# A hybrid decoder layer on one core: work of GpSimd in the fronts and the last stage put on VectorE and ScalarE, the S5 columns reordered by the gelu, and the merge's gate loads put ahead or on GpSimd's queue

## The chip, the core and the metric

The kernel runs on one core of a Trainium2 chip. A core has TensorE (PE, with its weight loads PEld), VectorE (DVE), ScalarE (ACT), GpSimd (POOL) and SyncE (SP), which issues most transfers. Each engine runs its instructions in the order in which they stand in its program. The metric is the device time in microseconds of one execution.

## What is computed

One layer of a decoder trunk on x of 1024 positions by 1024 channels, float32. Two token-mixing branches, a gated merge, and a gated MLP with a short convolution:

```python
h = rms_norm(x, norm_mix_pre)
proj = h @ w_in
p_rwkv, u_s5, gates = split(proj)          # gates = sigmoid(. + b_gate)
o_rwkv = rwkv7_branch(p_rwkv, ...) @ w_branch_rwkv
o_s5 = s5_branch(u_s5, ...) @ w_branch_s5  # ends: y = gelu(y); y * sigmoid(y @ w_glu + b_glu)
mixed = (g_rwkv * o_rwkv + g_s5 * o_s5) @ w_out
x = x + rms_norm(mixed, norm_mix_post)
f = conv_ffn(rms_norm(x, norm_ffn_pre), w_up, conv_w, conv_b, w_down)
x = x + rms_norm(f, norm_ffn_post)
```

The RWKV-7 branch is a recurrence over positions per head, with decay, key k, value v, receptance r and two vectors made from the normalised key; the S5 branch is a diagonal complex scan. A sigmoid is written as a tanh throughout, so a gate is (t + 1) times the product, with a factor of a half folded elsewhere.

## The kernel before

**Tiling.** Channels stand on the 128 partitions, positions in the columns. The sequence is worked in two halves of 512 positions, th = 0 and th = 1. Every large product is made of three float32r matmuls (`mm3_steps`, L172 to L174): the high part of the data by the high part of the weights, low by high, and high by low. The splits are made by a cast on ACT (L226, L156) and a difference on VectorE (L227, L157).

**Order.** TensorE's order is made by hand: a planner (`drive`) puts generators beside each other, and a `yield` in one of them names a modelled duration (the constants T_...), after which its next TensorE step may come. What is not a chain's own step is "fill": wide matmuls of the projections, gates and up-products that are put between. The order of the other engines and queues is made by the framework from priorities, as the data allow.

**The stages, in the time of the profiled run.** The input projection runs first; the RWKV fronts and chains and the S5 scans run beside it and beside the merge: the first half's fronts from about 262 to 322 us, the second half's from 478 to 560, the first half's merge from about 575, and the second half's from about 736 to 830. Up-products and convolution follow to about 1190, the down-product after that, and the outputs at the end.

**A front** (`rwkv_front`, L642 to L735) prepares one group of two units, of 128 channels each, for the chain; a half has two groups, so there are four group fronts in all. Per unit it loads k, tz and ta, then makes four 128x512 arrays: `bk0`, `bk1` (L670, L671, L690, L692, L701, L704) and `ar0`, `ar1` (L691, L702). It takes the key's norm by a small matmul (L677) that ends in `sv` (L682, L683), is spread by ACT (L688) and transposed by TensorE into `kb` (L698). L684 is a running sum over 64 columns, L686 and L687 are its Exps. Then the mask products: four matmul blocks per group (two units, two halves q, L716), each into a pair of PSUM buffers `cz`. There are two such pairs, so a block's matmuls wait until the block two before it has been emptied by VectorE's masked evictions into `gr` (L719, two per block). After the last one the products go out to memory through GpSimd's queue (L728) and come back for an inversion (L773 to L796), and a bonus product is made (L723, L734).

**The chain's end** transposes the result (L916), and ACT scales it into `ld` (L920); it is combined with the gate `TG` and stored as `YR` (L926).

**S5's end** (`s5_y`, `s5_split`, `glu_tile`). YU is loaded with its columns in the order j, n (8 by 64). ACT takes the gelu in place (L1092). The order n, j is needed, so the split's cast (L1097) and difference (L1098) and the product behind the GLU (L1108) work through a strided view.

**The merge.** `gate` (L1111 to L1118) loads the weights `w_br` and the gate `GT` (L1115), makes the product (PSUM `gm` or `mm`), and VectorE multiplies (L1118). `merge` does it for th = 0; `merge_s5` and `merge_rk` for th = 1, where `merge_rk` first loads the chain's `YR` (L1211). These loads are issued on SP's queue, among the loads of weights (L155) and of x (L1230).

**The last stage.** The outputs of th = 0 are made while the down-product's last part runs: ACT scales into a stage buffer (L1604), GpSimd multiplies by the norm (L1605) and adds the residual (L1606). Those of th = 1 come at the end, on VectorE (L1602, and L1606 for five of eight) and GpSimd (L1606 for three).

Of the kernel before, what the change touches and what calls it, by code (L numbers as in the profile page):

```python
# [66 lines left out]
class Kern:  # L67
# [574 lines left out]
    def rwkv_front(self, d, g, th, pt, start):  # L642
# [25 lines left out]
        for e in L:  # L668
            p = e["p"]
            G.tensor_scalar(e["bk1"], c64(e["ta"]), self.ka_h[:, p:p + 1], self.ka_1[:, p:p + 1], ALU.mult, ALU.add)  # L670
            G.tensor_tensor(e["bk1"], e["bk1"], c64(e["k"]), ALU.mult)  # L671
            A.activation(e["kk"], e["k"], AF.Square, scale=self.vec("k_k", p))
# [6 lines left out]
        for u, e in enumerate(L):  # L679
            p, tz = e["p"], e["tz"]  # L680
# [3 lines left out]
            V.tensor_tensor_scan(tz, self.cst("smask"), tz, 0.0, ALU.mult, ALU.add)  # L684
# [3 lines left out]
            A.copy(c64(e["yb"]), y.unsqueeze(2).to_broadcast([128, 8, 64]))  # L688
# [4 lines left out]
            e["r"] = ld(self.RKV[p])  # L693
# [5 lines left out]
        for e in L:  # L699
            r, tz = e["r"], e["tz"]  # L700
            V.scalar_tensor_tensor(e["bk0"], e["bk0"], -0.5, c64(e["kb"]), ALU.mult, ALU.mult)  # L701
            G.tensor_tensor(e["ar1"], c64(r), e["pe"][:, :, 1:65], ALU.mult)  # L702
            G.tensor_tensor(c64(r), c64(r), e["bk1"], ALU.mult)
            G.tensor_tensor(e["bk1"], e["bk1"], c64(tz), ALU.mult)  # L704
# [188 lines left out]
    def rwkv_out(self, ds, th, latency):  # L893
# [18 lines left out]
        for g, d in enumerate(ds):  # L912
# [14 lines left out]
            yield 1.0, 2.5  # L927
# [57 lines left out]
    def shifted_into(self, xs, mt):  # L985
# [3 lines left out]
        def use(th, ps):  # L989
            y = self.shifted(ps, mt, th)  # L990
            if mt == 12:
                nc.scalar.activation(y[0:64], y[0:64], AF.Tanh)
            else:
                nc.scalar.activation(y, y, AF.Tanh, scale=0.5)
                nc.gpsimd.tensor_scalar(y, y, 1.0, 0.5, ALU.add, ALU.mult)
# [4 lines left out]
    def lowrank(self, xs, js):  # L1000

        nc = self.nc
        for j, hb, dst in js:
            w = self.load_w(self.a["w_lr"][j])
            for th in range(2):
                for p in range(4):
# [7 lines left out]
                    if dst is self.TZ:  # L1014
                        nc.gpsimd.tensor_scalar(t, t, 1.0, 1.0, ALU.add, ALU.mult)
# [73 lines left out]
    def s5_y(self, t, b, th):  # L1089

        self.nc.sync.dma_start(t, self.YU[b].rearrange("j c g n -> (c g) j n")[:, :, th * 64:th * 64 + 64])
        self.nc.scalar.activation(t, t, AF.Gelu_apprx_tanh)  # L1092
        return t.rearrange("p j n -> p n j")

    def s5_split(self, hi, lo, y):
        r = [x.rearrange("p (n j) -> p n j", j=8) for x in (hi, lo)]
        self.nc.scalar.copy(r[0], y)  # L1097
        self.nc.vector.tensor_tensor(r[1], y, r[0].bitcast(F32), ALU.subtract)  # L1098

    def glu_tile(self, m, xs, t, y, to):  # L1100
# [5 lines left out]
        t3 = t.rearrange("p (n j) -> p n j", j=8)  # L1106
        nc.scalar.activation(t, ps, AF.Tanh, bias=self.hb["b_glu"][:, m:m + 1], scale=0.5)
        nc.vector.scalar_tensor_tensor(t3, t3, 1.0, y(), ALU.add, ALU.mult)  # L1108
        self.split_half(*to, t)

    def gate(self, j, m, th, br, t, out):  # L1111
# [3 lines left out]
        nc.sync.dma_start(t, self.GT[8 * j + m][:, th * 512:th * 512 + 512])  # L1115
# [15 lines left out]
    def merge(self, mg):  # L1131
# [11 lines left out]
        def inputs():  # L1143
# [808 lines left out]
```

## Time and profile before

| what | us |
|---|---|
| median of 3 runs | 1551.08 |
| lowest and highest of them | 1547.18, 1552.98 |
| the profiled execution, whole | 1552.89 |
| its span in the trace | 1551.1 |
| TensorE busy in it | 1460.4 |
| VectorE busy | 1081.2 |
| ScalarE busy | 687.0 |
| GpSimd busy | 161.1 |

All times of single instructions are from this one profiled execution. A row of a timeline has the start, the duration, the engine, the line, the operation, the tiles it writes and reads, its shape, how many alike are drawn together, and in brackets how long the engine stood idle before it and on what. A row of waits has the total, how often, and the longest. The matmuls of TensorE overlap, so the duration of one (0.39 us for 128x512) is longer than the distance from one start to the next.

### The profile page before, as it was taken

To read this page: it belongs to the slowest core of one execution; us is meant where nothing else is said; L and a number is where in the kernel's file an instruction comes from. 1 tells how busy PE (TensorE), PEld (TensorE's weight loads), DVE (VectorE), ACT (ScalarE), POOL (GpSimd) and SP (SyncE) were. 2 spreads that over 40 slices of the span, in tenths; PEclk is the share of its full clock that TensorE was granted. 3 is DMA by queue.
4 is the path that set the end of the run, shared out by engine and by line. 5 is a ranking of instruction groups with operands and counts; after the bars stand their busy time and mean duration, and the time that the engine had idled before them with its cause. 6 is when DMAs were issued, how large, how long until landed. Compare 5 with 4: busy or idle time off the path is not lost.

```text
span 1551.1 us, 24273 instructions
## 1 busy us (share of the span) xinstructions
PE 1460.4 (94%) x9332; PEld 1194.8 (77%) x9332; DVE 1081.2 (70%) x1733; ACT 687.0 (44%) x1069; POOL 161.1 (10%) x180
## 2 busy tenths in 40 slices
PE   5999899999999798999898999999999999999995
PEld 4787788778878586777776888788888887888774
DVE  6898784745326549447786689777777777697765
ACT  5354442433323444436444446444444444444361
POOL 2120100620103410100000000000000000000006
PEclk9999999999999899899998999999999999999997
DMA  6163342633513464523874444222222226944712
GB/s 208 41 203 118 93 127 100 196 115 113 153 44 107 153 190 143 144 69 94 255 245 161 153 144 137 103 82 82 82 84 88 87 82 203 334 149 134 241 59 108
DMA packets 131107, 210.45 MB, mean 136 GB/s; under 512 B 37696, under 2 KB 43840, under 8 KB 130992
## 3 DMA queue, kind: packets, MB, share of 16 engines
q1 hardware_dynamic: 124208, 188.32, 38.3%
q0 software_dynamic: 5632, 18.49, 3.7%
q10 hardware_dynamic: 1152, 2.10, 0.4%
q8 instruction: 73, 1.20, 0.3%
q14 instruction: 42, 0.34, 0.1%
HBM read 153.28 MB, written 53.48 MB: 133 GB/s over the span
## 4 chain that ended last, share of the span: by engine, by line
PE 69%; DVE 12%; DMA 8%; issue 5%; ACT 4%; POOL 1%; SPq 0%; DVEq 0%; ACTq 0%; POOLq 0%
PE gm L172 8%; PE gm L173 8%; PE gm L174 7%; PE rp L1382 4%; PE rp L1383 4%; PE rp L1384 4%; DMA st<-in_w_down_dram 2%; PE mm L1383 2%; PE mm L1382 2%; PE mm L1384 2%; PE ch L172 2%; PE ch L173 2%; PE ch L174 2%; PE d L1557 2%; PE d L1556 2%
## 5 line engine op out<-in xcount | busy, mean ns | idle before, releaser
L172 PE MATMUL gm<-hh,wh 128*128 128x512 f32 x688 | 284.7, 414 | 14.2 <-DVE hl L1118 8.8
L173 PE MATMUL gm<-hl,wh 128*128 128x512 f32 x688 | 273.4, 397 | 0.2 <-DVE hl L227 0.2
L174 PE MATMUL gm<-hh,wl 128*128 128x512 f32 x656 | 260.0, 396 | 0.0
L157 DVE TENSOR_TENSOR wl<-wf,wh 128x512 fp32r<-128x512 f32 x175 | 123.1, 705 | 116.1 <-ACT wh L156 108.1
L156 ACT CAST wh<-wf 128x512 fp32r<-128x512 f32 x179 | 110.5, 619 | 209.6 <-PE gm L173 129.4
L172 PEld LDWEIGHTS gm<-hh,wh 128*128 128x128 f32 x688 | 132.2, 192 | 49.0 <-DVE hl L1118 10.9
L173 PEld LDWEIGHTS gm<-hl,wh 128*128 128x128 f32 x688 | 132.3, 192 | 26.3 <-issue 1.0
L174 PEld LDWEIGHTS gm<-hh,wl 128*128 128x128 f32 x656 | 125.6, 191 | 27.5
L1557 PE MATMUL d<-xl,wh 128*128 128x512 f32 x308 | 120.2, 390 | 3.5 <-DVE xl L227 3.5
L1556 PE MATMUL d<-xh,wh 128*128 128x512 f32 x308 | 120.1, 390 | 2.1 <-ACT xh L226 2.1
L1558 PE MATMUL d<-xh,wl 128*128 128x512 f32 x308 | 119.9, 389 | 0.0
L1382 PE MATMUL rp<-t,h 128*128 128x512 f32 x216 | 84.4, 391 | 1.4 <-ACT p L1396 1.4
L1384 PE MATMUL rp<-t,l 128*128 128x512 f32 x216 | 84.2, 390 | 0.5 <-DVE l L227 0.5
L1383 PE MATMUL rp<-t,h 128*128 128x512 f32 x216 | 84.1, 389 | 0.0
L1557 PEld LDWEIGHTS d<-xl,wh 128*128 128x128 f32 x308 | 57.8, 188 | 16.5 <-DVE xl L227 4.8
L1556 PEld LDWEIGHTS d<-xh,wh 128*128 128x128 f32 x308 | 57.8, 188 | 14.5 <-ACT xh L226 2.5
L1558 PEld LDWEIGHTS d<-xh,wl 128*128 128x128 f32 x308 | 57.8, 188 | 12.0
L226 ACT CAST h<-r 128x1024 fp32r<-128x1024 f32 x34 | 35.8, 1054 | 61.1 <-PE rp L1383 32.5
L227 DVE TENSOR_TENSOR l<-r,h 128x1024 fp32r<-128x1024 f32 x34 | 41.6, 1224 | 29.2 <-ACT h L226 27.7
L1403 DVE SCALAR_TENSOR_TENSOR y<-zv,vecs,y 128x1023 f32<-128x1023 f32 (+1 forms) x36 | 46.1, 1280 | 8.5 <-ACT y L1401 8.5
L1382 PEld LDWEIGHTS rp<-t,h 128*128 128x128 f32 x216 | 40.5, 188 | 10.8 <-ACT p L1396 2.2
L1384 PEld LDWEIGHTS rp<-t,l 128*128 128x128 f32 x216 | 40.6, 188 | 9.4 <-DVE l L227 1.0
(458 smaller groups left out, 3269.8 us busy)
## 6 DMA issues: line engine op xcount, KB each, us to landing
r<-in_w_up_dram SPq DMA_DIRECT2D x36, 512.0 KB, 3.6
wf<-in_w_in_dram SPq DMA_DIRECT2D x68, 256.0 KB, 3.0
st<-in_w_down_dram SPq DMA_DIRECT2D x55, 256.0 KB, 4.3
st<-ACT SPq DMA_DIRECT2D x44, 256.0 KB, 4.4
wf<-in_w_up_dram SPq DMA_DIRECT2D x36, 256.0 KB, 2.7
ACT<-y POOLq DMA_DIRECT2D x18, 512.0 KB, 2.9
GT<-ev SPq DMA_DIRECT2D x32, 256.0 KB, 2.4
wf<-in_w_br_dram SPq DMA_DIRECT2D x32, 256.0 KB, 3.4
```

What stands on the lines that cost most here:

```text
L156: nc.scalar.copy(h[:, :n], f[:, :n])
L157: nc.vector.tensor_tensor(l[:, :n], f[:, :n], h[:, :n].bitcast(F32), ALU.subtract)
L172: mm(ps, a, xh[k], start=k == 0, stop=False)
L173: mm(ps, a, xl[k], start=False, stop=False)
L174: mm(ps, b, xh[k], start=False, stop=k == n - 1)
L1382: mm(ps, wh[:, c], xh, start=first and k == 0, stop=False, skip_group_check=True)
L1383: mm(ps, wh[:, c], xl, start=False, stop=False, skip_group_check=True)
L1384: mm(ps, wl[:, c], xh, start=False, stop=k == 3, skip_group_check=True)
L1403: V.scalar_tensor_tensor(y[:, lag:], z[:, 0:1024 - lag], self.vec(nme, i), y[:, lag:], ALU.mult, ALU.add)
L1556: mm(ps, wh[:, c], xh[:, x], start=start, stop=False, skip_group_check=True)
L1557: mm(ps, wh[:, c], xl[:, x], start=False, stop=False, skip_group_check=True)
L1558: mm(ps, wl[:, c], xh[:, x], start=False, stop=stop, skip_group_check=True)
```

## The change

Six edits, of one kind or another:

1. In `rwkv_front` the GpSimd operations go: L670 becomes an Identity with scale and bias on ACT, L671 and L702 to L704 go to VectorE. The running sum is moved ahead, the load of r one step ahead, and the spread of the norm (`yb`) ahead of the two Exps. T_BK, the modelled time between the transposes of the norm and the mask products, falls from 7 to 5 us.
2. In the input projection the GpSimd operations L995 and L1015 go to VectorE and ACT.
3. The gelu writes its result in the reordered columns into a buffer of its own; the splits and the product behind the GLU are contiguous. In the first half's merge the four S5 inputs are made in two steps of two.
4. The loads of the gates get a high priority, and for the second half's RWKV gates they are issued on GpSimd's queue, and so are the loads of `YR`.
5. In the last stage the outputs are made in place. Those of th = 0 are made on VectorE alone, six tiles while the last part's evictions start and two after it.
6. The chain's end at th = 1 yields 6.0 in place of 2.5 us of modelled time.

```diff
         for e in L:
-            p = e["p"]
-            G.tensor_scalar(e["bk1"], c64(e["ta"]), self.ka_h[:, p:p + 1], self.ka_1[:, p:p + 1], ALU.mult, ALU.add)
-            G.tensor_tensor(e["bk1"], e["bk1"], c64(e["k"]), ALU.mult)
-            A.activation(e["kk"], e["k"], AF.Square, scale=self.vec("k_k", p))
+            A.activation(e["kk"], e["k"], AF.Square, scale=self.vec("k_k", e["p"]))
+            e["r"] = ld(self.RKV[e["p"]])
+        for e in L:
+            p, tz = e["p"], e["tz"]
+            V.tensor_tensor_scan(tz, self.cst("smask"), tz, 0.0, ALU.mult, ALU.add)
+            A.activation(e["bk1"], c64(e["ta"]), AF.Identity, bias=self.ka_1[:, p:p + 1], scale=self.ka_h[:, p:p + 1])
+            V.tensor_tensor(e["bk1"], e["bk1"], c64(e["k"]), ALU.mult)
         yield 0, T_SQ
...
             V.scalar_tensor_tensor(e["bk0"], e["bk0"], -0.5, c64(e["kb"]), ALU.mult, ALU.mult)
-            G.tensor_tensor(e["ar1"], c64(r), e["pe"][:, :, 1:65], ALU.mult)
-            G.tensor_tensor(c64(r), c64(r), e["bk1"], ALU.mult)
-            G.tensor_tensor(e["bk1"], e["bk1"], c64(tz), ALU.mult)
+            V.tensor_tensor(e["ar1"], c64(r), e["pe"][:, :, 1:65], ALU.mult)
+            V.tensor_tensor(c64(r), c64(r), e["bk1"], ALU.mult)
+            V.tensor_tensor(e["bk1"], e["bk1"], c64(tz), ALU.mult)
...
-            yield 1.0, 2.5
+            yield 1.0, 6.0 if th else 2.5
...
-                nc.gpsimd.tensor_scalar(y, y, 1.0, 0.5, ALU.add, ALU.mult)
+                nc.vector.tensor_scalar(y, y, 1.0, 0.5, ALU.add, ALU.mult)
...
-                        nc.gpsimd.tensor_scalar(t, t, 1.0, 1.0, ALU.add, ALU.mult)
+                        nc.scalar.activation(t, t, AF.Identity, bias=self.ones1, scale=1.0)
...
-        self.nc.scalar.activation(t, t, AF.Gelu_apprx_tanh)
-        return t.rearrange("p j n -> p n j")
+        self.nc.scalar.activation(y.rearrange("p (n j) -> p j n", j=8), t, AF.Gelu_apprx_tanh)
+        return y
...
-        nc.sync.dma_start(t, self.GT[8 * j + m][:, th * 512:th * 512 + 512])
+        with self.tc.high_priority(HPW):
+            (nc.gpsimd if th and not j else nc.sync).dma_start(t, self.GT[8 * j + m][:, th * 512:th * 512 + 512])
...
-            if i == 0:
-                inputs()
+            if i < 2:
+                inputs((2 * i, 2 * i + 1))
...
-            nc.sync.dma_start(y, self.YR[k][:, 512:1024])
+            nc.gpsimd.dma_start(y, self.YR[k][:, 512:1024])
...
-        def outputs(th, src, bc, xs):
-            G = nc.gpsimd
+        def outputs(th, src, bc, xs, part=range(NK)):
             for n, m in enumerate(OUTORD[th]):
-                y = stage(0)[:, 0:512]
-                if th:
-                    V.scalar_tensor_tensor(y, src[m], self.vec("g_ffn_post", m), bc, ALU.mult, ALU.mult)
-                else:
-                    A.activation(y, src[m], AF.Identity, scale=self.vec("g_ffn_post", m))
-                    G.tensor_tensor(y, y, bc, ALU.mult)
-                (V if th and n not in (0, 2, 4) else G).tensor_tensor(y, y, xs[m], ALU.add)
+                if n not in part:
+                    continue
+                y = src[m]
+                V.scalar_tensor_tensor(y, y, self.vec("g_ffn_post", m), bc, ALU.mult, ALU.mult)
+                (nc.gpsimd if th and n in (0, 2, 4) else V).tensor_tensor(y, y, xs[m], ALU.add)
                 nc.sync.dma_start(self.out[m * 128:m * 128 + 128, th * 512:th * 512 + 512], y)
...
-T_KN, T_BK, T_GR, T_NF, T_MT, T_INV, T_LV, T_CH = 7.0, 7.0, 4.0, 5.0, 8.0, 43.0, 1.0, 0.8
+T_KN, T_BK, T_GR, T_NF, T_MT, T_INV, T_LV, T_CH = 7.0, 5.0, 4.0, 5.0, 8.0, 43.0, 1.0, 0.8
```

In the rows of the new order the line numbers are those of the changed file: a front's lines and those of the chain's end stand 2 or 3 higher (L719 is L721, L690 is L693, L682 is L684), the products L671 and L702 to L704 are L675 and L704 to L706, L1115 is L1113 and L1211 is L1213. The order on an engine is set by the planner and the framework, so the diff alone doesn't tell what moves. First, VectorE in the first half's first group, at its mask evictions (before L719, now L721; each pair of `cz` is one block, `ld_`, `bk_591` and `ar_28` belong to the second group's front). Before:

```order
L719 TENSOR_TENSOR gr_2593<-cz_2836,csts 128x4x128
L719 TENSOR_TENSOR gr_2593<-cz_2837,csts 128x4x128
L719 TENSOR_TENSOR gr_2593<-cz_2856,csts 128x4x128
L719 TENSOR_TENSOR gr_2593<-cz_2857,csts 128x4x128
L157 TENSOR_TENSOR wl_3157<-wf_3158,wh_3156 128x512
L978 SCALAR_TENSOR_TENSOR ev_2905<-gm_2823,vecs,ev_2905 128x511
L982 SCALAR_TENSOR_TENSOR ev_2905<-last,vecs,ev_2905 128x1
L719 TENSOR_TENSOR gr_2593<-cz_2929,csts 128x4x128
L719 TENSOR_TENSOR gr_2593<-cz_2930,csts 128x4x128
L719 TENSOR_TENSOR gr_2593<-cz_2949,csts 128x4x128
L719 TENSOR_TENSOR gr_2593<-cz_2950,csts 128x4x128
```

Now, with the first block's pair (cz_2827 and cz_2828) some rows above:

```order
L704 TENSOR_TENSOR ar_2867<-ld_2957,gr_2869 128x8x64
L693 SCALAR_TENSOR_TENSOR bk_591_2868<-ld_2882,ld_2874 128x8x64
L705 TENSOR_TENSOR ld_2957<-ld_2957,bk_591_2868 128x512
L695 SCALAR_TENSOR_TENSOR bk_591_2868<-bk_591_2868,vecs,ld_2878 128x8x64
L706 TENSOR_TENSOR bk_591_2868<-bk_591_2868,ld_2878 128x8x64
L721 TENSOR_TENSOR gr_2593<-cz_2902,csts 128x4x128
L721 TENSOR_TENSOR gr_2593<-cz_2903,csts 128x4x128
L721 TENSOR_TENSOR gr_2593<-cz_2847,csts 128x4x128
L721 TENSOR_TENSOR gr_2593<-cz_2848,csts 128x4x128
L721 TENSOR_TENSOR gr_2593<-cz_2922,csts 128x4x128
L721 TENSOR_TENSOR gr_2593<-cz_2923,csts 128x4x128
```

Before, the four blocks (unit 0's two, unit 1's two) are emptied in their order. Now the second block (cz_2847, cz_2848) is emptied behind the third (cz_2902, cz_2903) and behind products of the second group's front.

Second, VectorE in the second half's first group, at the last of its four evictions and what stands before it now:

```order
L157 TENSOR_TENSOR wl_5532<-wf_5533,wh_5531 128x512
L684 TENSOR_SCALAR sv_5209<-rp_5199 128x8
L706 TENSOR_TENSOR bk_876_5083<-bk_876_5083,ld_5091 128x8x64
L685 RECIPROCAL sv_5209<-sv_5209 128x8
L684 TENSOR_SCALAR sv_5213<-rp_5204 128x8
L705 TENSOR_TENSOR ld_5172<-ld_5172,bk_876_5083 128x512
L685 RECIPROCAL sv_5213<-sv_5213 128x8
L706 TENSOR_TENSOR bk_876_5083<-bk_876_5083,ld_5093 128x8x64
L694 SCALAR_TENSOR_TENSOR ar_5082<-ld_5089,vecs,gr_5084 128x8x64
L695 SCALAR_TENSOR_TENSOR bk_876_5083<-bk_876_5083,vecs,ld_5093 128x8x64
L721 TENSOR_TENSOR gr_4729<-cz_5137,csts 128x4x128
L721 TENSOR_TENSOR gr_4729<-cz_5138,csts 128x4x128
```

Before, the last three of the four blocks were emptied together, behind a first few operations of the second group's front (L690 to L692). Now the first three come ahead of nearly all of that front, and the last comes behind it.

Third, the issue of loads in the second half's merge. Before, on SP:

```order
L1211 DMA t_1367_7829<-YR_114 128x512
L155 DMA wf_8244<-in_w_br_dram 128x512
L1230 DMA tx_8782<-in_x_dram 128x512
L1115 DMA t_1440_8106<-GT_75 128x512
L1115 DMA t_1447_8133<-GT_76 128x512
```

Now, on GpSimd's queue, where nothing else stands between the inversion's transfers and the up-product's:

```order
L1213 DMA t_1374_7827<-YR_111 128x512
L1213 DMA t_1377_7833<-YR_112 128x512
L1213 DMA t_1380_7839<-YR_113 128x512
L1213 DMA t_1383_7845<-YR_114 128x512
L1113 DMA t_1456_8122<-GT_75 128x512
L1113 DMA t_1463_8149<-GT_76 128x512
```

All twelve, four of YR and eight of GT, are issued one after the other there.

49 lines of the change are left out of this document (24 added, 25 removed).

## The prediction

> **What bounds the kernel now.** I read the busy times first, then the same by stretch, then TensorE's waits, then the timelines of the stretches where those waits fall.
>
> ```profile
> PE 1460.4 (94%) x9332; PEld 1194.8 (77%) x9332; DVE 1081.2 (70%) x1733; ACT 687.0 (44%) x1069; POOL 161.1 (10%) x180
> span 1551.1 us, 24273 instructions
> ```
>
> TensorE sets the time. Only its idle stretches, 1551.1 − 1460.4 = 90.7 us, can be won by an edit that takes no matmul away, and this one takes none. So the question is which idle stretches the edit touches. The windows view puts busy time beside each stretch (columns: the stretch, its length, PE, PEld, DVE, ACT, POOL busy, clock, DMA share, GB/s):
>
> ```profile
> 262.00:322.00 60.00, 56.45 (x366) 45.63 (x366) 40.39 (x63) 21.37 (x37) 35.80 (x33) 0.94 0.56 180
> 478.00:524.00 46.00, 40.02 (x306) 31.34 (x303) 40.18 (x71) 18.40 (x35) 20.73 (x20) 0.89 0.40 133
> 524.00:560.00 36.00, 33.08 (x282) 26.54 (x281) 12.19 (x21) 16.30 (x33) 10.95 (x13) 1.00 0.66 204
> 590.00:640.00 50.00, 41.07 (x253) 32.12 (x253) 39.42 (x78) 16.89 (x33) 5.76 (x9) 0.90 0.68 181
> 736.00:830.00 94.00, 80.99 (x331) 63.68 (x330) 70.52 (x124) 38.35 (x66) 0.00 (x0) 0.89 0.72 232
> 1500.00:1551.00 51.00, 33.85 (x157) 28.36 (x155) 27.77 (x47) 11.89 (x16) 28.52 (x19) 0.79 0.22 83
> ```
>
> TensorE idles 3.6 us in the first half's fronts (262 to 322), 6.0 and 2.9 us in the second half's, 8.9 us in the first merge, 13.0 us in the second merge, and 17.2 us at the tail. What it waited for, by line (total, times, longest):
>
> ```profile
> PE gm L172 <- DVE hl L1118: 8.8, 4, 3.9
> PE cz L716 <- DVE gr L719: 7.6, 5, 3.0
> PE mm L172 <- ACT t L231: 4.6, 2, 3.8
> PE rp L916 <- ACT ld L920: 3.7, 1, 3.7
> PE mm L172 <- ACT t L226: 2.7, 2, 2.2
> PE mm L173 <- DVE t L227: 0.9, 1, 0.9
> ```
>
> These 28.3 us are within reach. The rest is not touched: the conversions at the start, the norms, the down-projection's drain.
>
> **The fronts.** Each of four group fronts has two units. Of a unit, five GpSimd operations go: L670 becomes an ACT Identity, L671, L702, L703 and L704 become VectorE products. VectorE is in the path here through the mask evictions (L719), since a mask matmul waits for a PSUM buffer that L719 empties. The cheapest of the GpSimd lines (columns after the count: busy us, mean ns of one), with VectorE's eviction and L690 for comparison:
>
> ```profile
> L702 POOL TENSOR_TENSOR ar<-ld,gr 128x512 f32<-128x512 f32 x8 | 10.0, 1244 | 21.5 <-DMA ld<-RKV 11.2 <-ACT wh L156 8.8 <-DVE rsh L133 1.6
> L719 DVE TENSOR_TENSOR gr<-cz,csts 128x512 f32<-128x512 f32 x32 | 20.1, 680 | 8.4 <-PE cz L716 8.4
> L690 DVE SCALAR_TENSOR_TENSOR bk<-ld,ld 128x512 f32<-128x512 f32 x8 | 8.7, 1089 | 0.0
> ```
>
> VectorE does a 128x512 product in about 0.68 us where GpSimd takes 1.24 or more. It gets 4 x 2 x 4 = 32 more: 32 x 0.68 = 21.8 us, 5.4 per group. ACT gets 8 more at about 0.7 us, 5.6 in all, which hides: ACT is busy 21.4 of 60 and 18.4 of 46 us there. Against the 21.8 stands a return. L690's mean is 1.09 us, yet the one at 480.09 takes 0.69; the timeline of the second half's first group shows where the difference comes from:
>
> ```profile
> 480.09 0.69 DVE L690 SCALAR_TENSOR_TENSOR bk<-ld,ld 128x512 f32<-128x512 f32 x1
> 511.10 1.16 DVE L690 SCALAR_TENSOR_TENSOR bk<-ld,ld 128x512 f32<-128x512 f32 x1
> 512.18 0.68 DVE L719 TENSOR_TENSOR gr<-cz,csts 128x512 f32<-128x512 f32 x1
> 512.78 0.74 DVE L692 SCALAR_TENSOR_TENSOR bk<-bk,vecs,ld 128x512 f32<-128x512 f32 x1
> 513.44 1.75 DVE L690 SCALAR_TENSOR_TENSOR bk<-ld,ld 128x512 f32<-128x512 f32 x1
> 517.04 1.28 DVE L719 TENSOR_TENSOR gr<-cz,csts 128x512 f32<-128x512 f32 x2
> 512.98 1.66 POOL L671 TENSOR_TENSOR bk<-bk,ld 128x512 f32<-128x512 f32 x1
> ```
>
> The L690 at 513.44 lasts 1.75 us, and GpSimd's product of 512.98 to 514.64 lies over most of it. Over eight L690 the stretch is 8 x (1.09 − 0.69) = 3.2 us. Were the other VectorE operations of a unit's front (L684, L691, L692) stretched as much, it would be 4 x 3.2 = 12.8 us. So VectorE's net load rises by 9 to 19 us over the four fronts.
>
> Second half, first group. TensorE waits there for the evictions:
>
> ```profile
> 511.32 0.40 PE L716 MATMUL cz<-ar,bk 64*64 64x128 f32 x2 [1.81 <-DVE gr L719]
> 512.91 1.98 PE L716 MATMUL cz<-ar,bk 64*64 64x128 f32 x30 [1.19 <-DVE gr L719]
> 517.87 2.58 PE L716 MATMUL cz<-ar,bk 64*64 64x128 f32 x32 [2.97 <-DVE gr L719]
> 309.45 0.43 PE L716 MATMUL cz<-ar,bk 64*64 64x128 f32 x2 [1.44 <-DVE gr L719]
> ```
>
> 1.8 + 1.2 + 3.0 = 6.0 us. In the new order three of this group's evictions stand ahead of the second group's front operations, not between them, which takes these waits away. The fourth now stands after about fifteen of the second group's front operations, some 10 us of VectorE work, where five or six stood before. It is needed not by a mask matmul but by the transfers of the mask products (L728), so by the inversion behind, which then is late by about 3 us (an estimate: ten operations more, 6.8 us, less VectorE's idle time before). Bounds −6.0 and +4; I take −2, since the order is fixed and the late eviction has TensorE's fill matmuls before it.
>
> First half, first group. In the new order the eviction of unit 0's second product comes after that of unit 1's first. Unit 1's second mask product waits for that buffer, so TensorE stands for the four evictions, 4 x 0.62 = 2.5 us (the pairs take 1.28), where it had 1.44. If unit 1's front operations, which stand ahead of both, are late too, it waits up to 6.4 us (eight products at 0.68 plus the rest of an eviction). The mask matmuls also come nine wide matmuls, 2.05 us at 0.227 each (an estimate from the spacing of starts), earlier in TensorE's order (T_BK from 7 to 5), which makes an eviction on VectorE look later by as much. Bounds −1.6 and +6.4; I take +3.
>
> **The first merge.** The four strided splits (L1098) become contiguous and are spread over two gates, and L1108 too.
>
> ```profile
> 593.84 1.02 DVE L1098 TENSOR_TENSOR hl<-ld,hh 128x512 fp32r<-128x512 f32 x1
> 595.10 0.69 DVE L1118 SCALAR_TENSOR_TENSOR hl<-ev,gm 128x512 f32<-128x512 f32 x1
> 610.75 0.50 PE L172 MATMUL gm<-hh,wh 128*128 128x512 f32 x1 [1.18 <-DVE hl L1118]
> 631.51 0.69 DVE L1118 SCALAR_TENSOR_TENSOR hl<-ev,gm 128x512 f32<-128x512 f32 x1 [2.53 <-DMA ev<-GT]
> ```
>
> The gate's product at 595.10 stands behind four splits of about 1.05 us. With two of 0.69 ahead of it, it comes 4.2 − 1.4 = 2.8 us sooner. L1108 falls from 1.07 to 0.69, −0.4 at each of two waits. The waits for a late gate load (2.53) get a higher rank, but the loads also wait for one of few buffers, so I give −0.8. Sum −4.4, taken as −4; bounds 0 and −8.8 (all of L1118's waits). The strided side moves into the gelu on ACT: a strided ACT write is nearest to L1097, 1.13 us where a contiguous cast takes 0.62, so 16 x 0.5 = 8 us on ACT, against 8 x 0.5 = 4 that the casts give back. ACT is busy 16.9 of 50 us, so it is covered, if not at the first gelu.
>
> **The second merge.** ACT's second L920 is late because two gelus that wait for their data stand before it:
>
> ```profile
> 738.79 0.63 ACT L1092 ACTIVATE et<-et 128x512 f32<-128x512 f32 x1 [1.38 <-DMA et<-YU]
> 742.66 0.77 ACT L920 ACTIVATE ld<-rp,vecs 128x512 f32<-128x512 f32 x1
> 743.48 0.66 PE L916 MATMUL rp<-csts,mt 128*128 128x128 f32 x4 [3.69 <-ACT ld L920]
> ```
>
> The new order has that pair of L920 adjacent, and the next pair with only one gelu between. −3, bounds 0 and −3.7. Then the loads: YR (L1211) and GT (L1115) stand on SP's queue between weight loads and land late.
>
> ```profile
> 786.65 0.48 SPq L1211 DMA_DIRECT2D t<-YR  x1
> 817.45 0.43 SPq L1115 DMA_DIRECT2D t<-GT  x1
> 819.64 0.69 DVE L1118 SCALAR_TENSOR_TENSOR t<-t,mm 128x512 f32<-128x512 f32 x1 [1.05 <-DMA t<-GT]
> L1337 POOL DMA_DIRECT2D ACT<-y x18 | 9.6, 532 | 337.9 <-DVE y L1336 337.9
> ```
>
> They move to GpSimd's queue, which is empty here (POOL busy 0.00 in the row of 736 to 830): 12 issues at about 0.53 us, 6.4 us, done once YR is written and buffers are free. The waits for them are 2.7 + 0.9 (YR's split) and 4.6 (L231, behind the gate of 819.64), 8.2 us together. I take −6. Bounds: −8.2, and +2 where the loads come all at once into a stretch whose DMA share is 0.72 already and push weight loads back.
>
> **The rest.** L1015 and L995 leave GpSimd in the input projection: −0.5, bounds 0 and −2. At the tail, the outputs of the first half go to VectorE, 12 operations of 0.7 us before its last squares, for which it has room (27.8 busy of 51 us); the stage buffers go, and with them this wait near the end:
>
> ```profile
> 1543.52 1.41 DVE L1602 SCALAR_TENSOR_TENSOR st<-q,vecs,d 128x512 f32<-128x512 f32 x2 [0.94 <-DMA out_dram<-st]
> ```
>
> −1.5: 0.94, a stretched sum, and a last squares chain not held up; bounds 0 and −2.
>
> **The sum.** −2 + 3 − 4 − 3 − 6 − 0.5 − 1.5 = −14. The profiled execution took 1552.89 (its span 1551.1 and 1.8 around it), so 1538.9; the median of the runs is 1551.08, 1.8 lower, so **1537**. All low ends give −32, all high ones +12.
>
> **Rivals.** (A) *The evictions queue behind the added products*, and the change is slower. Each group puts 8 products, 5.4 us, on the engine that empties the mask's PSUM; if in all four fronts they fall ahead of an eviction that TensorE stands for, that costs 4 x 5.4 = 21.6 less the waits' stretch (2 us): +19.6, in place of +1, against −15 elsewhere: +4.6, so 1556. It decides from 15 / 4 = 3.8 us per front. For it: 40.2 of 46 us busy on VectorE. Against it: 40.4 of 60 in the first half's fronts, and three evictions moved forward.
> (B) *The loads are not sooner*: buffers hold the first merge's, contention eats the second's. The merges then give −1 − 2 and L920 −3: sum −2 + 3 − 1 − 3 − 2 − 2 = −7, 1544. For it: a DMA share of 0.68 and 0.72; against it: GpSimd's empty queue.
> (C) *GpSimd's silence frees VectorE wholly*: the fronts give −1.6 − 6.0, the first merge −6, the rest as forecast less one: −7.6 − 6 − 3 − 7 − 2 = −25.6, 1525. For it: the 1.75 us L690; against it: 21.8 us of new products.
> [...]
>
> **Chances.** Forecast 0.48, A 0.16, B 0.22, C 0.14. A time within 0.5% (7.8 us) of before can't be told from no change. The forecast is faster by more in nine of ten cases, C in all, B in four of ten, A in none, and A is slower by more in four of ten: faster 0.43 + 0.14 + 0.09 = 0.66, slower 0.07, same the remaining 0.27. The range goes from C's 1525 (half of C, 0.07, lies below) to A's 1556 (half of A, 0.08, lies above), and holds the costs' bounds between.
>
> **What would show it.** Right: no wait of TensorE for L226 of YR's split or for L231 in the second merge; the 3.7 us at L916 gone; L1118's total below 5 us; L690 at 0.69 in the fronts; a new wait of 2 to 3 us at a mask matmul in the first half's first group. Wrong: waits for mask evictions above 10 us in all (A), weight casts waiting for w_br loads in the second merge (B), or no wait for evictions at all (C).

## The result and the profile after

| what | before | after |
|---|---|---|
| median of 7 runs each, us | 1549.11 | 1543.38 |
| lowest and highest | 1546.93, 1552.98 | 1540.52, 1545.26 |
| span of the profiled execution | 1551.1 | 1543.5 |

The ratio is 0.9958, with an interval from 0.9944 to 0.9972: about 6.5 us faster. The interval leaves out 1, but 0.42% is still under the half per cent below which the prediction would not tell a change from none. The way was right, the time lies in the range, and the size is less than half of the 14 us that were forecast.

The waits of TensorE after the change, longest groups of those that answer to the ones shown before (total, times, longest; the new lines stand 2 or 3 higher in the front, L1118 is L1116):

```profile
PE mm L172 <- ACT t L231: 6.2, 3, 3.2
PE gm L172 <- DVE hl L1116: 5.8, 4, 2.1
PE cz L718 <- DVE gr L721: 5.5, 3, 4.4
PE mm L172 <- ACT mx L1263: 3.9, 1, 3.9
PE rp L822 <- issue: 2.8, 1, 2.8
PE cz L747 <- ACT bk L756: 2.6, 1, 2.6
```

The waits for ACT's scaling of the chain's end (L920, 3.7 us) and for YR's split (2.7 and 0.9) are gone from the list. But the wait at the second merge's end (L231) grew from 4.6 to 6.2, and the waits at L1263, L747 and the 2.8 us at L822 are new or larger. The same stretches by busy time:

```profile
262.00:322.00 60.00, 52.66 (x336) 41.66 (x334) 42.54 (x74) 23.32 (x39) 5.52 (x13) 0.91 0.52 175
478.00:524.00 46.00, 44.15 (x395) 35.34 (x390) 37.41 (x77) 21.50 (x41) 1.43 (x6) 1.00 0.35 116
736.00:830.00 94.00, 81.23 (x337) 64.34 (x337) 65.81 (x120) 39.07 (x65) 6.43 (x12) 0.91 0.68 216
```

TensorE loses 7.3 us in the first half's fronts, where it lost 3.6. It loses 1.9 where it lost 6.0 in the second half's first front. And the window of the second merge, in which 9 us were to be won, has it busy for 81.2 us, as before (81.0).

Windows at fixed times mix what moved. The trace also gives the start of the n-th matmul. Where two kernels have executed the same set of matmuls up to the n-th, the difference of the two starts says how much was won or lost until there. So a table by stage (time in the kernel before, and the difference of others to it, with a dash where the sets differ; three of the experiments stand beside the change and are told below):

```
stage ends (start of the same matmul)        before   after   evict   T_BK 7  T_BK 5 alone
second group's work before the fronts' masks  284.0    -1.2    -0.5    -2.5    +0.3
first half, first group's mask products       315.2    +3.9    -3.8    +1.8    +2.0
first half's chain                            480.4    +8.7    +6.5    +6.3    +7.3
second half's fronts                          559.1    +7.2    +8.8    +7.6    +9.8
first merge, second half's chain              712.8    -0.8    -0.3    +0.1    +1.8
second merge's beginning                      743.9    -5.3    -4.9       -    -2.8
second merge, S5 gates under way              769.9    -1.2    -0.8    +2.0    +2.3
second merge, first RWKV gate                 785.1    -1.2    -0.8    +4.5    +2.3
second merge, RWKV gates under way            796.4    -8.4    -8.0    +4.3    -4.9
second merge's end                            830.4    -4.0    -3.7    +4.7    -2.7
up-product                                   1112.3    -4.0    -3.3    +5.2    -2.5
down-product's last matmul                   1527.4    -2.0    -3.9    +7.5    +1.1
norm of the last outputs                     1537.1    -5.6    -7.9    +4.5    +0.4
end of the span                              1551.1    -7.6    -9.8    +2.5    +0.4
```

After the change TensorE is 7 us *behind* when the fronts are over, wins 8 in the first merge and beside the second half's chain, wins and loses several times in the second merge, and wins its last 5.6 us at the tail. Each column is one execution, counted from the start of its span, and in the down-product (1112.3 to 1527.4) a column shifts by 0.6 to 3.6 us, one way or the other, so single rows are read for their steps of several us only.

### The profile page after: what moved, and what is told of

Read it like the earlier page. It is cut to its first block, busy times and chain, and to the rows that moved or that the text cites. A ratio compares the mean times of both kernels' runs of the same rounds, so it can differ in the third digit from the quotient of the medians.

```text
span 1543.5 us, 24191 instructions
## 1 busy us (share of the span) xinstructions
PE 1455.5 (94%) x9332; PEld 1191.3 (77%) x9332; DVE 1084.8 (70%) x1783; ACT 696.9 (45%) x1077; POOL 74.0 (5%) x126
## 4 chain that ended last, share of the span: by engine, by line
PE 76%; DVE 10%; DMA 6%; ACT 4%; issue 3%; SPq 0%; POOL 0%; ACTq 0%; DVEq 0%; POOLq 0%
PE gm L172 9%; PE gm L173 8%; PE gm L174 8%; PE rp L1384 4%; PE d L1559 4%; PE d L1558 4%; PE rp L1385 4%; PE rp L1386 4%; PE d L1560 4%; PE mm L1384 2%; PE mm L1386 2%; PE mm L1385 2%; PE ch L172 1%; PE ch L173 1%; PE ch L174 1%
## 5 line engine op out<-in xcount | busy, mean ns | idle before, releaser
L1558 PEld LDWEIGHTS d<-xh,wh 128*128 128x128 f32 x308 | 58.2, 189 | 15.9 <-ACT xh L226 2.5
L1559 PEld LDWEIGHTS d<-xl,wh 128*128 128x128 f32 x308 | 58.2, 189 | 15.8 <-DVE xl L227 3.9
```

Of the source, the lines that this page charges most:

```text
L1558: mm(ps, wh[:, c], xh[:, x], start=start, stop=False, skip_group_check=True)
L1559: mm(ps, wh[:, c], xl[:, x], start=False, stop=False, skip_group_check=True)
```

## The experiments

All were timed against runs of the kernel before in the same series, on the same chip; 0.001 of the ratio is 1.55 us. The series differ in their chip, so two versions are compared by their ratios and intervals.

**The order of the evictions.**

```diff
-                for h in range(2):
-                    V.tensor_tensor(d["gr"][:, u, 4 * q:4 * q + 4, h], ps[h], gm, ALU.mult)
+                with self.tc.high_priority(HPW):
+                    for h in range(2):
+                        V.tensor_tensor(d["gr"][:, u, 4 * q:4 * q + 4, h], ps[h], gm, ALU.mult)
```

> The changed kernel, with the mask evictions at a high priority, so that VectorE empties the four blocks in their order. Theory (the 5 us that the first half's first front lost come from the second block being emptied behind the third and behind the second group's products): the wait of 4.5 us for an eviction goes, TensorE reaches the end of that front 4 to 5 us sooner, and the time falls by 3 to 5 us, to about 1539. Rival (the front lost because the mask products were put two us earlier in TensorE's order, and the engine as a whole is full): the wait moves to another eviction, and the time stays within 1.5 us of 1543.

Measured: 1542.28, ratio 0.9935 (0.9911 to 0.9958). In the changed kernel, TensorE (first row) and VectorE (the others) stand like this in the first half's front:

```profile
311.81 2.58 PE L718 MATMUL cz<-ar,bk 64*64 64x128 f32 x32 [4.44 <-DVE gr L721]
310.46 0.68 DVE L706 TENSOR_TENSOR bk<-bk,ld 128x512 f32<-128x512 f32 x1
311.07 2.48 DVE L721 TENSOR_TENSOR gr<-cz,csts 128x512 f32<-128x512 f32 x4
```

The evictions start after the second group's last product, and TensorE waits 4.4 us. With the evictions at a high rank the mask products of both blocks run through without a bracket:

```profile
305.41 2.43 PE L718 MATMUL cz<-ar,bk 64*64 64x128 f32 x64
```

TensorE is 7.7 us earlier than in the changed kernel at the end of that group. But by the end of the fronts nothing of it is left (+8.8 against +7.2). It is lost at three places: 3.2 us between 312 and 322 us, where TensorE waits 1.3 us for VectorE (L680) and then has half its clock from 317.3 to 320.7; 2.2 us in the inversion, where the clock is half for 10.2 us in place of 6.8; and 3.8 us between 519 and 548, where the longest wait is one of 4.2 us for VectorE, at L700. The medians differ by 1.1 us, the ratios by 0.0023, with intervals that overlap. The order of the evictions makes the wait; the wait is worth little here.

**The loads as before.**

```diff
-        with self.tc.high_priority(HPW):
-            (nc.gpsimd if th and not j else nc.sync).dma_start(t, self.GT[8 * j + m][:, th * 512:th * 512 + 512])
+        nc.sync.dma_start(t, self.GT[8 * j + m][:, th * 512:th * 512 + 512])
...
-            nc.gpsimd.dma_start(y, self.YR[k][:, 512:1024])
+            nc.sync.dma_start(y, self.YR[k][:, 512:1024])
```

> The changed kernel, with the loads of YR and of the gates on SyncE's queue at the old rank. Theory (the earlier loads take 7 us of waits away in the second merge, but its end waits for VectorE, which gives 4.4 us of that back; and the high rank of the gate loads makes weights late ahead of it): the waits for YR's split of about 3.6 us come back, those at the merge's end shrink to under 7 us, and the time rises by only 0 to 3 us. Rival (the loads' gain is kept in full): 1543 + 7, about 1550.

Measured: 1543.79, ratio 0.9949 (0.9927 to 0.9971), the same as the change. The time was near what the theory had, but not for its reason: the waits for YR's split did *not* come back. In the SyncE queue the last load of YR is issued here at

```profile
767.77 0.33 SPq L1212 DMA_DIRECT2D t<-YR  x1
```

which is 7.6 us ahead of the first RWKV gate's first matmul (775.40). Before, on the same queue, it was at 786.65, 2.7 us behind that matmul (783.99). What starts these loads is the store. The last stores of YR before the change and in this run:

```profile
764.02 0.32 SPq L926 DMA_DIRECT2D YR<-ld  x1
748.69 0.32 SPq L928 DMA_DIRECT2D YR<-ld  x1
```

In both, the first of the four loads follows 3 us behind (767.00 and 751.86), and the others stand between weight and x loads over the next 16 to 20 us. What differs is the lead of the last store over the gate: 20.0 us before, 26.7 us here, 27.8 us in the changed kernel (stored at 754.94). On GpSimd's queue, in the changed kernel, the four are issued within 2 us (758.65 to 760.29), much sooner than the gate needs them. So not the queue, but the chain's place in TensorE's order took these waits away.

**T_BK at 7 again.**

```diff
-T_KN, T_BK, T_GR, ... = 7.0, 5.0, 4.0, ...
+T_KN, T_BK, T_GR, ... = 7.0, 7.0, 4.0, ...
```

> The changed kernel, with T_BK at 7 again. This puts the mask products nine wide matmuls later in each group and the last chain's end 36 wide matmuls (8 us) later. Theory (the second merge's waits for YR went because YR was stored 9 us sooner, by the chain's earlier place in TensorE's order, and not by the queue of its loads, which with the loads on SyncE as before were gone too): waits for the split of YR of 2 to 4 us come back, and the time rises by 2 to 5 us, less 1 to 2 that the later mask products save in the first half's front: 1544 to 1547. Rival (the modelled time only moves fill about): no such waits, and the time within 1.5 us.

Measured: 1555.59, ratio 1.0018 (1.0002 to 1.0035). Without this one number the change is *slower* than before: 0.0060, or 9.3 us, hang on it, where 1 to 4 us were expected. The waits at the first RWKV gates are back, though the loads stand on GpSimd's queue:

```profile
788.12 0.47 PE L172 MATMUL mm<-t,wh 128*128 128x512 f32 x1 [1.92 <-issue]
791.86 0.79 PE L173 MATMUL mm<-t,wh 128*128 128x512 f32 x1 [1.28 <-DVE t L227]
793.67 0.79 PE L172 MATMUL mm<-t,wh 128*128 128x512 f32 x1 [0.59 <-ACT t L226]
795.53 0.79 PE L173 MATMUL mm<-t,wh 128*128 128x512 f32 x1 [1.06 <-DVE t L227]
```

The table has the step: from 785.1 to 796.4 the change wins 7.2 us, and with T_BK at 7 only 0.2. But it is not YR's store that is late, as the theory had it: the last load of YR is issued at 768.62, 19.5 us ahead of the first of these matmuls. ACT's casts stand behind weight casts, and those wait for the loads of w_br on SyncE's queue:

```profile
780.00 0.62 ACT L156 CAST wh<-wf 128x512 fp32r<-128x512 f32 x1 [5.85 <-DMA wf<-in_w_br_dram]
787.41 0.62 ACT L156 CAST wh<-wf 128x512 fp32r<-128x512 f32 x1 [4.19 <-DMA wf<-in_w_br_dram]
787.93 0.61 ACT L226 CAST t<-t 128x512 fp32r<-128x512 f32 x1
```

TensorE's matmul at 788.12 follows the weight cast that ends at 788.03. Why the later chain makes these loads late is not shown. The waits for mask evictions rise too, from 5.5 to

```profile
PE cz L718 <- DVE gr L721: 14.2, 4, 5.7
```

but at the end of the fronts the two kernels are within 0.5 us of each other (+7.6 and +7.2).

**T_BK at 5 alone**, in the kernel before.

```diff
-T_KN, T_BK, T_GR, ... = 7.0, 7.0, 4.0, ...
+T_KN, T_BK, T_GR, ... = 7.0, 5.0, 4.0, ...
```

> The kernel before the change, with T_BK at 5 and nothing else. Theory (the number alone carries most of the gain, as the changed kernel without it fell to 1.0018 of the time before: it stores YR sooner and the second merge stops waiting for it): waits for YR's split go, the time falls by 4 to 9 us, to 0.994 to 0.997. Rival (the number and the fronts' products need each other: with the products on GpSimd, 1.2 to 1.6 us each, the mask products that come 2 us sooner wait for them): TensorE waits for evictions or mask products more than 12 us in all, as in the run with the products back on GpSimd, and the time stays within 3 us of before.

Measured: 1553.42, ratio 1.0008 (0.9993 to 1.0024): no gain. The number and the other edits need each other, as the rival said, but not for its reason: the evictions cost less than before (7.6 us), not more.

```profile
PE cz L716 <- DVE gr L719: 4.7, 5, 2.9
PE mm L172 <- ACT t L231: 4.7, 3, 2.7
PE mm L172 <- ACT mx L1261: 4.7, 1, 4.7
```

YR's waits did go (the last column wins 7.2 us between 785.1 and 796.4; YR's last store is at 755.14), but TensorE, 2.8 us ahead at 743.9, lost 5.1 us by 769.9, and 2.2 at the merge's end. What is left, 2.7 us at 830.4, is lost in the down-product of this execution, and the tail's gain is missing here. Why the same number pays 9 us beside the other edits and nothing without them is shown only this far.

**T_BK at 4.**

```diff
-T_KN, T_BK, T_GR, ... = 7.0, 5.0, 4.0, ...
+T_KN, T_BK, T_GR, ... = 7.0, 4.0, 4.0, ...
```

> The changed kernel with T_BK at 4: the mask products come 4 to 5 wide matmuls sooner still in each group, the last chain's end 24 rows. Theory (once the second merge no longer waits for YR, an earlier chain wins nothing there, and the mask products meet their evictions and products later on VectorE): between the same and 3 us slower, the wait for mask evictions above 5.5 us. Rival (the chain's place in the order goes on paying, 9 us for the step from 7 to 5, so some 4 for the next): faster by 3 to 5 us.

Measured: 1546.04, ratio 0.9959 (0.9944 to 0.9973): the change's own. The gain ends at 5. Mask evictions cost 5.3 us, about as in the change, not more. TensorE now waits 11.5 us in one piece at the second merge's first gate, for a copy on ACT that stands behind two weight casts; these wait 3.24 and 6.75 us for loads of w_br:

```profile
PE mm L172 <- ACT mx L1263: 11.5, 1, 11.5
762.44 0.62 ACT L156 CAST wh<-wf 128x512 fp32r<-128x512 f32 x1 [6.75 <-DMA wf<-in_w_br_dram]
```

**The chain's end yields 2.5 us.**

```diff
-            yield 1.0, 6.0 if th else 2.5
+            yield 1.0, 2.5
```

> The changed kernel, with the chain's end at the second half yielding 2.5 us as before, so that its last two transposes stand 15 wide matmuls (3.4 us) sooner. Theory (ACT's scaling of the transposes, L922, is the wait that the longer yield covers): TensorE waits 3 to 4 us for ACT at the last transposes, the time rises by 0 to 3 us, since 4 us of the earlier kernel's gain there were lost again at the merge's first gate, where weights came late. Rival (the longer yield only delays YR): faster by 1 to 2 us.

Measured: 1542.75, ratio 0.9943 (0.9924 to 0.9963). No wait of 3 to 4 us for ACT at the last transposes appeared, against the theory (1.0 us at L918, 0.7 in the change), and nothing in time that can be told from the change.

**The outputs as before.**

```diff
-                y = src[m]
-                V.scalar_tensor_tensor(y, y, self.vec("g_ffn_post", m), bc, ALU.mult, ALU.mult)
-                (nc.gpsimd if th and n in (0, 2, 4) else V).tensor_tensor(y, y, xs[m], ALU.add)
+                y = stage(0)[:, 0:512]
+                if th:
+                    V.scalar_tensor_tensor(y, src[m], self.vec("g_ffn_post", m), bc, ALU.mult, ALU.mult)
+                else:
+                    A.activation(y, src[m], AF.Identity, scale=self.vec("g_ffn_post", m))
+                    G.tensor_tensor(y, y, bc, ALU.mult)
+                (V if th and n not in (0, 2, 4) else G).tensor_tensor(y, y, xs[m], ALU.add)
...
```

> The changed kernel, with the last stage's outputs as before: ScalarE and GpSimd, through stage buffers. Theory (GpSimd's products beside VectorE's last squares stretch them, which holds up the last sum of squares by 3.6 us, and the buffers hold the last outputs by 2): slower by 4.5 to 6.5 us, about 1549. Rival (the tail is bound by the chain of sum, root, product and store anyway; what was forecast): slower by 1 to 2 us.

Measured: 1548.35, ratio 0.9989 (0.9971 to 1.0008): 0.0031, or 4.8 us, come from the outputs, as the theory said and the forecast did not, though the two intervals just touch (0.9971 and 0.9972). TensorE's sum of squares, before, with these outputs put back, and after the change (one row of each timeline), then a square's sum on VectorE with the outputs put back:

```profile
1529.36 4.97 PE L245 MATMUL d<-ones,sq 128*128 128x1 f32 x24 [1.60 <-DVE sq L1508]
```

```profile
1525.26 4.33 PE L245 MATMUL d<-ones,sq 128*128 128x1 f32 x24 [1.60 <-DVE sq L1510]
1522.49 1.05 DVE L1510 TENSOR_TENSOR sq<-sq,sq 128x512 f32<-128x512 f32 x1 [0.82 <-ACT sq L1584]
```

```profile
1525.76 2.93 PE L245 MATMUL d<-ones,sq 128*128 128x1 f32 x24
```

24 small matmuls take 5.0 us and a wait of 1.6 where the squares come late beside GpSimd's products, and 2.9 us without a wait where GpSimd is idle. VectorE's sums of squares are stretched to 1.05 and 1.16 us, against 0.69 after the change. The longer run of the matmuls themselves is the granted clock: it falls to half at 1529.7 us before the change and at 1526.3 with the outputs put back, among these matmuls, whose starts then stand 0.21 us apart in place of 0.11. After the change it falls at 1528.4, when the last of them has started. The wait for a stage buffer near the end (0.95 us here) is there again too.

**The products on GpSimd again.**

```diff
-            V.tensor_tensor(e["ar1"], c64(r), e["pe"][:, :, 1:65], ALU.mult)
-            V.tensor_tensor(c64(r), c64(r), e["bk1"], ALU.mult)
-            V.tensor_tensor(e["bk1"], e["bk1"], c64(tz), ALU.mult)
+            G.tensor_tensor(e["ar1"], c64(r), e["pe"][:, :, 1:65], ALU.mult)
+            G.tensor_tensor(c64(r), c64(r), e["bk1"], ALU.mult)
+            G.tensor_tensor(e["bk1"], e["bk1"], c64(tz), ALU.mult)
```

(and the product with k likewise)

> The changed kernel, with the fronts' four products per unit back on GpSimd; the rest of the fronts as changed. Theory (the products on VectorE cost the first half's first front 5 us by the order of evictions and win 1 to 2 in the second half): faster by 0 to 4 us. Rival (VectorE gains more from GpSimd's silence than it loses by the products): slower by 3 to 8 us, with mask evictions waited for about 7 us as before the change.

Measured: 1546.94, ratio 0.9969 (0.9951 to 0.9986): 1.7 us slower than the change, between the two expectations and with an interval that overlaps. The first half's front does end earlier, 2.0 us ahead of before; the second half's fronts lose 9.6 us (from +6.2 at 480.4 to +15.8 at 559.1), where the change wins 1.5. Mask evictions cost

```profile
PE cz L718 <- DVE gr L721: 12.0, 4, 7.3
```

**S5's columns as before.**

```diff
-        self.nc.scalar.activation(y.rearrange("p (n j) -> p j n", j=8), t, AF.Gelu_apprx_tanh)
-        return y
+        self.nc.scalar.activation(t, t, AF.Gelu_apprx_tanh)
+        return t.rearrange("p j n -> p n j")
...
-            if i < 2:
-                inputs((2 * i, 2 * i + 1))
+            if i == 0:
+                inputs()
...
```

> The changed kernel, with the gelu in place and the splits and the GLU product strided again, and the four S5 inputs made at one gate. Theory (the first merge's gain, 5.9 us from the fronts' end to its first gate and some 4 behind, is that of the contiguous splits): VectorE's gate product waits behind four splits of 1.05 us again, the waits of TensorE for it go from 5.8 to about 9 us, and the time rises by 3 to 5 us, to about 1547. Rival (TensorE came to the merge late, by the fronts' loss, so that VectorE had caught up anyway): it rises by less than 1.5 us.

Measured: 1542.18, ratio 0.9934 (0.9916 to 0.9952): the S5 edit brings nothing, if it does not cost a little. The rival holds: the strided kernel passes the first merge as the contiguous one does, from +6.3 at 559.1 to −4.0 at 712.8.

**Evictions and loads in one.**

The two diffs above together.

> The changed kernel with the evictions at a high priority and the loads of YR and the gates as before: the two single edits in one. Theory (the parts add up: the eviction order is worth 2 to 4 us, the loads' place nothing): 1539 to 1542, TensorE's wait for mask evictions under 1 us, and no wait for YR's split. Rival (what one part wins, the next stretch loses, as the evictions' 7 us in the first half's front were mostly lost by the end of the fronts): 1543 to 1545.

Measured: 1539.79, ratio 0.9920 (0.9899 to 0.9940). This version beats the kernel before by about 12 us. Against the change the ratios differ by 0.0038, about 6 us, but the two intervals only just miss each other (0.9940 and 0.9944), and the next two versions, which contain this pair, overlap with the change; so that it is faster than the change is likely, and its size open. TensorE's wait for mask evictions falls to 0.2 us, and there is none for YR's split, as the theory said.

**The same and S5's columns as before.**

> The changed kernel with three edits undone or mended: evictions at a high priority, loads of YR and gates as before, the S5 columns strided as before. What is left of the change are the fronts, T_BK, the last stage and the input projection. Theory (S5's and the loads' edits give nothing, the eviction order costs 3 to 4): at or below the 1540 of the run with evictions and loads alone, 0.989 to 0.992. Rival (the S5 edit is worth its 4 us once the waits ahead of the first merge are gone): 0.994 to 0.996.

Measured: 1539.60, ratio 0.9929 (0.9905 to 0.9953). No better than the pair: what is left of the change here, the fronts, T_BK, the longer yield, the outputs and the input projection, carries all of its gain, with the evictions put in order.

**The pair and the shorter yield.**

> The changed kernel with evictions at a high priority, loads of YR and gates as before, and the chain's end at the second half yielding 2.5 us: the best pair so far and the one other edit whose undoing came out faster. Theory (the second merge is held by the weights at its first gate and by VectorE at its end, so a chain that ends a little sooner adds nothing to the pair): 0.991 to 0.993, as the pair's 0.9920. Rival (the three parts add up, 2.3 us more): 0.990 or lower, about 1536 where before is 1551.

Measured: 1540.26, ratio 0.9939 (0.9918 to 0.9960). The parts do not add up; the rival falls. The ratio lies above the theory's 0.991 to 0.993, but its interval covers nearly all of that.

## Why the prediction came out as it did

**What bounds it.** TensorE sets the time and no matmul was taken away: right. The step that failed is the one under the whole sum, that a wait which goes is time won. The waits for L920's scaling and for YR's split went whole (7.3 us), those at L1118 and for the mask evictions in part (8.8 to 5.8, 7.6 to 5.5), and L231's grew. But behind each wait that went stood another engine or load that was as late, and the next wait took most of the time.

**The second merge (forecast −3 and −6, found −3.2 in all: −0.8 at 712.8, −4.0 at 830.4).** Mis-sized, and for the larger part with the wrong cause. The 3.7 us at L916 went, and TensorE was 5.3 us ahead at 743.9. Then it waited for ACT, which stood behind a weight cast (ACT's first two rows, TensorE's third):

```profile
755.08 0.62 ACT L156 CAST wh<-wf 128x512 fp32r<-128x512 f32 x1 [3.97 <-DMA wf<-in_w_br_dram]
755.60 0.58 ACT L1263 COPY mx<-gm 128x512 f32<-128x512 f32 x1
756.23 0.50 PE L172 MATMUL mm<-e,wh 128*128 128x512 f32 x1 [3.91 <-ACT mx L1263]
```

4.1 of the 5.3 us were given back by 769.9. The waits for YR went, 7.2 us in all (3.6 us of waiting, and the matmuls behind it, for which the clock was half from 789.0 to 795.8 us before), but the prediction put that down to GpSimd's queue, and the loads on SyncE's do as well. It is T_BK that puts the last chain's end 36 wide matmuls, 8 us, sooner, of which the longer yield of edit 6 gives 15 back; alone, in the kernel before, it takes these waits away too. The prediction read these 36 rows' worth only as 2 us per group on the cost side in the fronts, and never asked what stands at the end of four groups. At the merge's end 4.4 us were lost again, to VectorE (VectorE's first two rows and the last, TensorE's third):

```profile
808.58 0.68 DVE L1116 SCALAR_TENSOR_TENSOR t<-t,ch 128x512 f32<-128x512 f32 x1
809.78 0.69 DVE L1220 TENSOR_TENSOR t<-t,e 128x512 f32<-128x512 f32 x1
811.34 0.61 PE L172 MATMUL mm<-t,wh 128*128 128x512 f32 x1 [3.24 <-ACT t L231]
816.29 0.16 DVE L265 TENSOR_SCALAR rv<-rp 128x4 f32<-128x4 f32 x1 [1.42 <-PE rp L245]
```

VectorE is busy for 15.9 of the 16 us from 798 to 814. The gate's product at 808.58 stands in its queue among the norm's products and weight splits, and a later one behind a small operation that itself waits for TensorE. TensorE came earlier, VectorE did not.

**The tail (−1.5, found −4.8 by experiment).** Right mechanism, mis-sized by three. The term counted the wait for a store (0.94), and left 0.56 us for a stretched sum and "a last squares chain not held up" together. The rows of L245 before and after say 1.6 of wait and 2.0 of its own length, the latter at half the clock, which the term did not have.

**The fronts (+1, found +8.4 from 284.0 to 559.1).** The first group's wait was forecast as 2.5 to 6.4 us, taken as 3; it is 4.4, and the mechanism is the forecast one. The second half's waits for evictions went, 6.0 us, and 5.7 us of other waits came (L680, L762, L747), so that this stretch wins 1.5 for the −2 expected. What was not seen is the 4.8 us lost between 315 and 480 (below). But the experiment on the order of evictions shows that little of the fronts' loss is lost for good.

**The first merge (−4, found about −8 from 559.1 to 712.8).** L1118's waits fell from 8.8 to 5.8 us, and to 6.9 with the columns strided as before, so the contiguous ones account for a third of that at most; and the strided kernel wins no less over the stage. T_BK at 5 alone, with none of the merge's edits, wins as much there (from +9.8 to +1.8), and so does every column of the table. All of them arrive 7 us or more later than before, so VectorE may have had time to catch up; this is argued from the table and not shown.

**What was to show it.** VectorE's product with k (L690, now L693) takes 0.684 us in the mean, as expected, and the waits at L916 and for YR's split are gone. L1118's total was to be below 5 us and is 5.8; L231's wait was to go and grew.

**The input projection (−0.5).** −1.2 at 284.0. The experiments that have its edits stand between −0.5 and −4.8 there, the one that has not at +0.3: the way fits, and the size can't be told.

**The rivals.** A, that evictions behind the products make the change slower, fell as a whole; with T_BK at 7 it comes closest to the truth (14.2 us of such waits, 1.0018), though there the larger loss is in the second merge. B, that the loads are not sooner, had the right time (it gave 1544) for partly the wrong reason: the loads are sooner, and it is worth nothing that can be told. Its sign, weight casts that wait for w_br loads, is there in the rows above. C fell: the fronts were not freed.

## What to carry to other kernels

A wait that goes is won only up to the next thing that is late; before summing waits, ask for each what the waiting engine meets next, and who is full there. Where a planner's number moves a chain against the fill, follow it to the end of the chain and not only to the stage in which it stands, and try it alone and left out: here it carried 9 us beside the other edits and none without them. An edit that is made of six parts is worth undoing one by one: the S5 columns, the loads' place and the longer yield were each worth nothing that could be told, and undoing the loads' place together with one small mend gave the lowest ratio of all, 0.9920. A wait can also come with a cost beyond its length: the granted clock fell to 0.50 within the wait of 2.2 us that ends at 790.39 us before the change, and within the one of 2.75 us that ends at 417.53 after it, stayed there for 6.8 us both times, and the wide matmuls behind started 0.43 us apart in place of 0.227.

## What was not expected of the hardware

**A wait in the middle of a burst.** In the changed kernel TensorE stops for 2.75 us among 128 small matmuls of the first half's inversion, and waits for nothing that the profile names:

```profile
413.85 0.93 PE L822 MATMUL rp<-ld,gr 32*32 32x32 f32 x48
417.53 0.64 PE L822 MATMUL rp<-ld,gr 32*32 32x32 f32 x16 [2.75 <-issue]
418.69 0.63 PE L173 MATMUL gm<-hl,wh 128*128 128x512 f32 x1
419.12 0.63 PE L174 MATMUL gm<-hh,wl 128*128 128x512 f32 x1
```

It is there, with 2.4 to 4.0 us, in every kernel with T_BK at 5, the kernel before with only that number changed among them. With T_BK at 4 and 7 among the new kernels a wait of that kind, 1.9 and 2.0 us, stands a little later, at L832; in the kernel before there is none here. The DMA view counts one packet of the queue of instructions between 408 and 414 us before the change,

```profile
q8 instruction: 1, 0.02, 1.2%
```

and none after it, where the next comes between 414.6 and 417.6:

```profile
q8 instruction: 1, 0.02, 2.0%
```

So TensorE may have run out of instructions: 320 weight loads and matmuls start from 411.7 to 414.8 us, and no packet of that queue between 385.6 and 415.1. The raw records bear this out further. 73 packets come for 18,664 weight loads and matmuls, 256 each in the mean. In each of the eleven kernels that wait here, 395 to 398 more of them have been started at this point than 256 for every packet so far, the most in the whole execution, and TensorE goes on 2.3 to 2.5 us after the next packet has started (415.1 in the changed kernel). This fits, but no run took it away, and it stays an inference.

**Half speed behind it.** The two wide matmuls above start 0.43 us apart, where they start 0.227 apart elsewhere; six of them run so, which costs 1.2 us more. The granted clock is 0.50 from 415.6 to 422.4 us and 1.00 just before (414.8 to 415.6); it falls 0.8 us after the wait begins at 414.8. From 411.7 us until the wait TensorE had run matmuls of 64 and 32 columns alone. Whether the clock answers to the wait, to these small matmuls or to both, no run shows.
